# Fourteen column pairs per layer in seven products, 31 pool tiles, and the accumulating loads issued at the fetch

## The chip, the cores and the metric

The kernel runs on one core of one Trainium2 chip. The metric is the device time of one execution in microseconds (us). Before the change it is 2264.33 us, the median of 3 runs (2263.88 to 2264.35).

## The reference

A trunk of two decoder layers works on 256 tokens of width 2048 in float32. Each layer is a mixer and then an MLP, each on a normalised input and each added to the residual:

```python
h = rms_norm(x, norm_mix[layer])
x = x + mixer(h)                      # layer 0: windowed attention and a state-space scan; layer 1: dilated attention
h = rms_norm(x, norm_ffn[layer])
u = h @ w_up                          # 2048 -> 8192
x = x + square(relu(u)) @ w_down      # 8192 -> 2048
```

The change lies in the two MLPs, above all in the product with `w_down`. The mixers compute the same as before.

## The kernel before

**Operands in two parts.** Every float32 operand is split into a high and a low part, and a product is made of three matmuls (high by high, high by low, low by high). ScalarE (ACT) makes the high part `whi` of a weight tile, VectorE (DVE) the low part `wlo` (`split`, and `high` and `low` in `run`). TensorE (PE) can start a tile when both are there.

**The plan.** All matrix work is one list, `plan`, of pieces. `run` (line 291) walks through it. At each piece it emits, in this order, `low` for the piece two ahead, `fetch` for the piece six ahead, `high` for the piece three ahead, and `add` for the piece four ahead, and then the matmuls. Small work (norms, relu, transposes, splits of `u`) is kept as side tasks that `tick` slips in between; `need` forces a task to its end where a piece cannot go on without it, and so puts its instructions right ahead of that piece's matmuls.

**Two kinds of pieces in the MLP.** Both take 256 rows (two k tiles) of a weight stripe 512 columns wide, which is one tile of 128 x 1024 values, 512 KB.
- A plain piece serves all 256 tokens, with 12 matmuls that are 512 columns wide. Its weight tile is `wraw`, with four buffers, loaded by SyncE's queue (SP).
- A seven piece belongs to a `Seven` (line 245). It computes, for a chunk `c` of 1024 rows of `w_down` and a pair of column stripes (a column pair), the two by two block product with seven products in the place of eight. Each product takes two pieces (halves `h`) of 6 matmuls. Blocks are called 11, 12, 21, 22 (row half, column half); the tokens are halved too. The seven are P1, P2, and Q3 to Q7.

A column pair of a chunk takes 96 matmuls in plain pieces and 84 as a `Seven`. The price of a `Seven` is sums. Sums of operand blocks (`s1`, `s2`, then `sh`, `sl`) are made once per chunk in `operands`. Sums of weight blocks are made in two ways: `add` lets DVE add two tiles (for Q6 and Q4), and `accumulate` has GpSimd's queue (POOL) issue a DMA that loads a block from `w_down` and adds it to a tile that is there already (block 12 onto tile 11 and block 22 onto tile 12, for both halves: four such DMAs per column pair). `evict` adds each finished product to the residual `res` (7 DVE additions of 128 x 512 per column pair).

**What sets the order before.** `LOADS` says which blocks a product fetches: P1 fetches 11, P2 fetches 21, 12 and 22, in SP's order. Both accumulating DMAs are issued from `low` (line 331): the one onto 11 follows the low part of P1, which is the last reader of the plain block 11, and the one onto 12 follows the low part of P2. Q6 comes third, and its sum needs tile 11 with its accumulation done.

**The chunks.** There are eight chunks per layer. `w_up` is consumed in 16 units of 8 plain pieces. After the first two units, each chunk's seven pieces are mixed with the following units' pieces by `mixed` (line 1036): `for c, n in enumerate((20, 20, 8, 20, 20, 24, 0))` gives each chunk `n` plain pieces, of which the first four or five come ahead of the seven pieces. Before, chunks 0, 1, 3, 4 and 5 take both column pairs as `Seven`; chunks 2 and 6 take one, and their other pair is done in plain pieces (`down`); chunk 7 is plain. That is 12 per layer.

**The tile pool.** `work` has 29 tiles of 4 KB per partition: weight blocks of the `Seven`s (`sraw`), `uf`, `uh`, `ul`, the sums, and all mixer tiles. A tile is taken again when its last reader is done.

Of the kernel before, what the change touches and what calls it, by code (L numbers as in the profile page):

```python
# [15 lines left out]
T = 256  # L16
# [4 lines left out]
W = 512  # L21
# [19 lines left out]
def trunk(ctx: ExitStack, tc: tile.TileContext, x, norm_mix, norm_ffn, w_up, w_down, ab_w_in, ab_q_norm,  # L41
# [48 lines left out]
    nc.scalar.preload_act_table(AF.Exp)  # L90
    cst = consts.tile([128, C_ALL], F32, name="cst")
    par0 = w4([32, 128], "par0")
# [39 lines left out]
    cbm = cst[:, C_CB:C_CB + 128]  # L132
    mask0 = cst[:, C_M0:C_M0 + 384]
    mask1 = cst[:, C_M1:C_M1 + 384]
    mult1 = cst[:, C_N1:C_N1 + 384]
    cwT = consts.tile([128, 96], F32, name="cwT")
# [98 lines left out]
    def unit(*a, **k):  # L235
# [3 lines left out]

    SEVEN = (("P1", "a", "11"), ("P2", "b", "21"), ("Q6", "a", "t2"), ("Q7", "c", "12"), ("Q5", "a", "11"),  # L240
             ("Q4", "c", "21"), ("Q3", "a", "22"))
    LOADS = {"P1": ("11",), "P2": ("21", "12", "22")}
    SUMS = {"Q6": ("t2", "11", "22"), "Q4": ("21", "21", "t2")}

    class Seven:


        def __init__(self, w, rows, c0, kts, operands, to, needs, mark):
            self.w, self.rows, self.c0, self.operands, self.to, self.needs, self.mark = \
                w, rows, c0, operands, to, needs, mark  # L250
# [8 lines left out]
        def fetch(self, p, h):  # L259
            for b in LOADS.get(SEVEN[p][0], ()):  # L260
                r, c = self.rows[int(b[0]) - 1] + h * KC, self.c0 + (int(b[1]) - 1) * W
                nc.sync.dma_start(self.tile(b, h),
                                  self.w[r * 128:(r + KC) * 128, c:c + W].rearrange("(k p) c -> p k c", p=128))

        def add(self, p, h):
# [4 lines left out]

        def accumulate(self, p, h):

            o = {"P1": ("11", 0), "P2": ("12", 1)}.get(SEVEN[p][0])
            if o is not None:
                r, c = self.rows[o[1]] + h * KC, self.c0 + W
                nc.gpsimd.dma_start(self.raw[o[0], h],  # L276
                                    self.w[r * 128:(r + KC) * 128, c:c + W].rearrange("(k p) c -> p k c", p=128),
                                    accum_op=OP.add)

# [3 lines left out]
        def evict(self, p):  # L283

            name, b, _ = SEVEN[p]
            t, j, op = {"P1": (0, 0, OP.add), "P2": (0, 0, OP.add), "Q6": (1, 0, OP.add), "Q7": (1, 1, OP.subtract),
                        "Q5": (1, 1, OP.subtract), "Q4": (1, 0, OP.add), "Q3": (0, 1, OP.subtract)}[name]
            r = self.to[t][j]
            V.tensor_tensor(r, r, self.bank[b], op=op)

    def run():
# [54 lines left out]
        high(AHEAD)  # L346
        nc.sync.dma_start(cst[:, C_TRI:], shapes[:, C_TRI:])
        pending = []
        before = ps = None
        kept, held = [], []  # L350
        for i, (u, c) in enumerate(todo):
# [9 lines left out]
            if isinstance(u, Seven):  # L361
# [7 lines left out]
                sp = u.bank[b]  # L369
                xh, xl, t0 = u.operands(name)  # L370
                tick(True)
                for k in range(KC):
                    q = h * KC + k
                    wh, wl = xh[:, q, t0:t0 + 128], xl[:, q, t0:t0 + 128]
                    PE.matmul(sp, wh, hi[:, k], start=new and k == 0, stop=False, skip_group_check=True)
# [247 lines left out]

    def residual_unit(w, ktiles, j, needs={}, nm=None, last=None, check=None, mark=None):
        def after(ps):
            if check is not None:
                check()
            add_stripe(ps, j, last)
            if nm is not None:
                nm.begin(j)  # L630
# [15 lines left out]
    v0 = consts.tile([128, 2, 2, 64], F32, name="v0")  # L646
    k0T = consts.tile([128, 2, T], F32, name="k0T")
    dt = consts.tile([128, 2, 32], F32, name="dt")
# [6 lines left out]
    cumd = dram.tile([32, 2, 128], F32, name="cumd")  # L655
    btok = consts.tile([128, 4, 128], F32, name="btok")
    dtx = small.tile([128, 2, 32], F32, name="dtx", bufs=1)
# [293 lines left out]
    def mlp(layer, nm, nxt, last=None):  # L951
# [60 lines left out]
        def down(c, j):  # L1012
# [5 lines left out]

            def whole():
                assert all(("down", layer, k, j) in done or ("down", layer, k, j - j % 2) in done for k in range(NC - 1))  # L1020

            return residual_unit(wd, kts, j, {4 * b: ("u", layer, 2 * c + b) for b in range(2)}, nxt, last, whole).pieces

        def seven(c, j):
            def parts(name):
                i, k, t = {"P1": (0, 0, 0), "P2": (0, 1, 0), "Q4": (0, 1, 128), "Q5": (1, 0, 0), "Q6": (1, 0, 128),
                           "Q7": (1, 1, 0), "Q3": (1, 1, 128)}[name]
                return (sums[c][k] if i else u[2 * c + k]) + (t,)

# [3 lines left out]
                         {0: ("u", layer, 2 * c), 1: ("u", layer, 2 * c + 1), 2: ("sums", layer, c)},  # L1033
                         marks[c][-1]).pieces

# [28 lines left out]
    oh, ol = [None] * 4, [None] * 4  # L1064

    def dilated(g):
        boxes = [[], []]
        vb = []

        def after_qk(i, ps):  # L1070
            side(heads_T(n2, ps, R_QK + 2 + i, "qk"[i], boxes[i]), ("qk", g, i))
            if i == 1:
# [99 lines left out]
```

## Time and profile before

| what | value |
|---|---|
| median of 3 runs | 2264.33 us |
| the profiled execution's own time | 2264.74 us |
| span of its instructions on the core | 2262.9 us |
| granted TensorE clock | 1.00 |
| TensorE matmul busy | 2247.2 us, 99% |
| VectorE busy | 1749.7 us, 77% |
| ScalarE busy | 1290.0 us, 57% |
| GpSimd busy (it only issues DMAs) | 125.7 us, 6% |
| moved by DMA | 475.10 MB, of it 50.48 MB by GpSimd's queue |

The span runs from the first instruction to the last; the 1.8 us between it and the execution's own time lie outside. `L71` stands for every instruction that goes through the recording helper at line 71, so groups are told apart by their tiles. A matmul of 512 columns is listed with 0.39 us, but matmuls overlap in the array, and the pitch from one to the next is what counts. `q0` is GpSimd's DMA queue, `q1` SyncE's. The first layer's MLP lies at about 480 to 1130 us, the second's at about 1570 to 2263 us.

### The profile page before, as it was taken

The numbers are of one execution on the slowest core, as the hardware profiler recorded it, in microseconds if no ns is written. First come the engines' busy times: TensorE is split into PE (matmuls) and PEld (weight loads), VectorE is DVE, ScalarE is ACT, GpSimd is POOL, SyncE is SP. The second block draws the span as 40 slices with busy tenths as digits, with TensorE's granted clock in tenths as the row PEclk, the third lists the DMA queues.
The fourth block names the chain that finished last, engine by engine and source line by source line (L and its number), as shares of the span: only waits on it lengthen the run. The fifth ranks groups of instructions, "written<-read, shape, count | busy, mean of one in ns | idle before, by whom it ended". The sixth has DMA issues, their size and how long they took to land.

```text
span 2262.9 us, 30235 instructions
## 1 busy us (share of the span) xinstructions
PE 2247.2 (99%) x11029; PEld 1873.0 (83%) x11029; DVE 1749.7 (77%) x2482; ACT 1290.0 (57%) x1615; POOL 125.7 (6%) x116
## 2 busy tenths in 40 slices
PE   8999999999999999999999999999999999999999
PEld 7998988888888888888788778778888888888877
DVE  6779986556888888887976766665588888888786
ACT  6565545445666556565664555555566665656663
POOL 1000000000001010000000000000000000010000
PEclk9999999999999999999999999999999999999999
DMA  7546555568797797888756455546788789797874
GB/s 235 163 142 190 177 177 182 190 186 246 216 296 214 209 288 222 242 245 234 219 171 192 149 158 168 168 151 186 245 237 240 206 242 281 207 282 228 248 222 141
DMA packets 255318, 475.10 MB, mean 210 GB/s; under 512 B 17156, under 2 KB 27696, under 8 KB 255168
## 3 DMA queue, kind: packets, MB, share of 16 engines
q1 hardware_dynamic: 218976, 416.34, 56.7%
q0 software_dynamic: 26624, 50.48, 12.5%
q10 hardware_dynamic: 9568, 6.34, 0.9%
q8 instruction: 86, 1.41, 0.2%
q14 instruction: 64, 0.52, 0.1%
HBM read 470.97 MB, written 2.13 MB: 209 GB/s over the span
## 4 chain that ended last, share of the span: by engine, by line
PE 97%; DMA 1%; DVE 1%; issue 1%; ACT 0%; SPq 0%; DVEq 0%; POOLq 0%; ACTq 0%
PE acc L71 71%; PE sp L71 20%; PE uT L71 1%; PE sc L71 1%; PE o L71 1%; DMA sraw<-in_w_down_dram 1%; PE pT L71 1%; PE yp L71 1%; PE xT L71 1%; DVE wlo L71 1%; DMA wraw<-in_ab_w_in_dram 0%; PE qp L71 0%; DMA res<-in_x_dram 0%; PE yo L71 0%; PE kp L71 0%
## 5 line engine op out<-in xcount | busy, mean ns | idle before, releaser
L71 ACT ACTIVATE whi<-wraw 128x1024 fp32r<-128x1024 f32 (+1 forms) x600 | 631.9, 1054 | 493.6 <-PE acc L71 350.8
L71 DVE TENSOR_TENSOR wlo<-wraw,whi 128x1024 fp32r<-128x1024 f32 (+1 forms) x600 | 725.0, 1214 | 233.7 <-PE acc L71 159.7
L71 PE MATMUL acc<-whi,hThi 128*128 128x512 f32 (+1 forms) x1632 | 647.7, 397 | 1.8 <-ACT hThi L71 1.7
L71 PE MATMUL acc<-whi,hTlo 128*128 128x512 f32 (+1 forms) x1632 | 634.8, 389 | 1.0 <-DVE hTlo L71 1.0
L71 PE MATMUL acc<-wlo,hThi 128*128 128x512 f32 (+1 forms) x1632 | 634.1, 389 | 0.7 <-DVE wlo L71 0.7
L71 ACT ACTIVATE whi<-sraw 128x1024 fp32r<-128x1024 f32 x336 | 353.7, 1059 | 292.4 <-DVE sraw L71 137.0
L71 DVE TENSOR_TENSOR wlo<-sraw,whi 128x1024 fp32r<-128x1024 f32 x336 | 408.8, 1221 | 85.3 <-PE acc L71 35.3
L71 PEld LDWEIGHTS acc<-whi,hThi 128*128 128x128 f32 x1632 | 307.6, 188 | 66.8 <-issue 5.8
L71 PEld LDWEIGHTS acc<-whi,hTlo 128*128 128x128 f32 x1632 | 307.2, 188 | 65.7 <-DVE hTlo L71 1.8
L71 PEld LDWEIGHTS acc<-wlo,hThi 128*128 128x128 f32 x1632 | 307.9, 189 | 60.9 <-DVE wlo L71 1.1
L276 POOL DMA_DIRECT2D sraw<-in_w_down_dram x96 | 117.3, 1576 | 2058.7 <-DVE wlo L71 1815.6
L71 PE MATMUL sp<-wlo,sh 128*128 128x512 f32 x384 | 149.5, 389 | 0.0
L71 PE MATMUL sp<-whi,sl 128*128 128x512 f32 x384 | 149.5, 389 | 0.0
L71 PE MATMUL sp<-whi,sh 128*128 128x512 f32 x384 | 149.4, 389 | 0.0
L71 DVE TENSOR_TENSOR sraw<-sraw 128x1024 f32<-128x1024 f32 x96 | 117.1, 1219 | 26.4 <-DMA sraw<-in_w_down_dram 26.3
L71 DVE TENSOR_TENSOR res<-res,sp 128x512 f32<-128x512 f32 x168 | 114.7, 682 | 17.4 <-PE sp L71 17.1
L71 PE MATMUL acc<-hThi,whi 128*128 128x256 f32 x384 | 112.3, 293 | 0.0
L71 PE MATMUL sp<-whi,ul 128*128 128x512 f32 x288 | 112.1, 389 | 0.0
L71 PE MATMUL sp<-whi,uh 128*128 128x512 f32 x288 | 112.0, 389 | 0.0
L71 PE MATMUL sp<-wlo,uh 128*128 128x512 f32 x288 | 112.0, 389 | 0.0
L71 PE MATMUL acc<-hThi,wlo 128*128 128x256 f32 x384 | 108.5, 283 | 0.0
L71 PE MATMUL acc<-hTlo,whi 128*128 128x256 f32 x384 | 108.5, 283 | 0.0
(221 smaller groups left out, 2749.8 us busy)
## 6 DMA issues: line engine op xcount, KB each, us to landing
wraw<-in_w_up_dram SPq DMA_DIRECT2D x256, 512.0 KB, 5.2
sraw<-in_w_down_dram SPq DMA_DIRECT2D x192, 512.0 KB, 8.1
wraw<-in_ab_w_in_dram SPq DMA_DIRECT2D x96, 512.0 KB, 3.7
sraw<-in_w_down_dram POOLq DMA_DIRECT2D x96, 512.0 KB, 10.7
wraw<-in_c_w_qkv_dram SPq DMA_DIRECT2D x96, 512.0 KB, 4.2
wraw<-in_w_down_dram SPq DMA_DIRECT2D x64, 512.0 KB, 4.2
wraw<-in_ab_w_out_dram SPq DMA_DIRECT2D x48, 512.0 KB, 3.7
wraw<-in_c_w_o_dram SPq DMA_DIRECT2D x32, 512.0 KB, 3.6
```

What stands on the lines that cost most here:

```text
L71: return f(out, *a, **k)
L276: nc.gpsimd.dma_start(self.raw[o[0], h], self.w[r * 128:(r + KC) * 128, c:c + W].rearrange("(k p) c -> p k c", p=128), accum_op=OP.add)
```

## The change

- Chunks 0 to 6 now take both column pairs as `Seven`, 14 per layer, and the plain pieces are spread as `(18, 17, 17, 18, 17, 17, 8)`. Chunk 7 stays plain, and the second pair of chunk 6 is mixed with it.
- Q7 and Q6 change places. P1 fetches blocks 12 and 11, P2 blocks 21 and 22. The accumulating DMA onto tile 12 is issued in `fetch`, right behind the load of tile 12; the one onto 11 stays behind the low part of P1.
- Of the even `u` block of chunks 0 to 6 only the first 128 tokens are split, with high and low part in one tile (`uhl`), since plain pieces no longer read it.
- The pool grows from 29 to 31 tiles. `cst` shrinks to 384 columns; the masks become pool tiles (`mask0`, and `masks`, which is loaded when layer 1's first attention unit is done), and `k0T` and `btok` become the two halves of a pool tile `kb`.
- A stripe's next norm (or its store) begins when both the last `Seven` and chunk 7's plain unit of that stripe are done (`early`, `ready`).

```diff
-    work = ctx.enter_context(tc.tile_pool(name="work", bufs=29))
+    work = ctx.enter_context(tc.tile_pool(name="work", bufs=31))
...
-    SEVEN = (("P1", "a", "11"), ("P2", "b", "21"), ("Q6", "a", "t2"), ("Q7", "c", "12"), ("Q5", "a", "11"),
+    SEVEN = (("P1", "a", "11"), ("P2", "b", "21"), ("Q7", "c", "12"), ("Q6", "a", "t2"), ("Q5", "a", "11"),
              ("Q4", "c", "21"), ("Q3", "a", "22"))
-    LOADS = {"P1": ("11",), "P2": ("21", "12", "22")}
+    LOADS = {"P1": ("12", "11"), "P2": ("21", "22")}
...
                 nc.sync.dma_start(self.tile(b, h),
                                   self.w[r * 128:(r + KC) * 128, c:c + W].rearrange("(k p) c -> p k c", p=128))
+                if b == "12":
+                    self.accumulate("12", 1, h)
...
-                if isinstance(u, Seven):
-                    u.accumulate(*c)
+                if isinstance(u, Seven) and c[0] == 0:
+                    u.accumulate("11", 0, c[1])
...
-            for k in marks[c - 1] if 0 < c < NC - 2 else [("up", layer)] if c else []:
+            for k in marks[c - 1] if 0 < c < NC - 1 else [("up", layer)] if c else []:
                 yield from until(k)
-            if c == NC - 1:
-                yield from until(("uf", layer, 2 * c + 1))
             for i in (2 * c, 2 * c + 1):
                 yield from until(("uf", layer, i))
-                u[i] = slot("uh"), slot("ul")
-                split(u[i][0], u[i][1], uf[i])
+                if i % 2 == 0 and c < NC - 1:
+                    u[i] = slot("uhl")
+                    split(u[i][:, :, :128], u[i][:, :, 128:], uf[i][:, :, :128])
+                else:
+                    u[i] = slot("uh"), slot("ul")
+                    split(u[i][0], u[i][1], uf[i])
...
-        for c, n in enumerate((20, 20, 8, 20, 20, 24, 0)):
+        for c, n in enumerate((18, 17, 17, 18, 17, 17, 8)):
             x, o = ups[o:o + n], o + n
+            s = seven(c, 0) + seven(c, 2)
             if c == NC - 2:
-                x = sum((down(c, j) for j in (0, 1)), []) + sum((down(c + 1, j) for j in range(NS)), [])
-                mixed(x, seven(c, 2), 2, 19)
-            elif n == 8:
-                mixed(x + down(c, 2) + down(c, 3), seven(c, 0), 4.5, 16)
+                mixed(x, s[:9], 4, n + 4)
+                mixed(sum((down(c + 1, j) for j in range(NS)), []), s[9:], 0, 15)
             else:
-                mixed(x, seven(c, 0) + seven(c, 2), 4.5, n + (3 if n == 24 else 0))
+                mixed(x, s, 4.5, n)
```

The first place is SP's queue, at the first column pair of chunk 1 in layer 0. Before, tile 6009 is block 11 of the first half, 6044 block 11 of the second; then follow 21, 12 and 22 of the first half (6066, 6068, 6070) and of the second (6121, 6123, 6125):

```order
L262 DMA sraw_6009<-in_w_down_dram 128x2x512
L306 DMA wraw_6021<-in_w_up_dram 128x2x512
L262 DMA sraw_6044<-in_w_down_dram 128x2x512
L262 DMA sraw_6066<-in_w_down_dram 128x2x512
L262 DMA sraw_6068<-in_w_down_dram 128x2x512
L262 DMA sraw_6070<-in_w_down_dram 128x2x512
L306 DMA wraw_6095<-in_w_up_dram 128x2x512
L262 DMA sraw_6121<-in_w_down_dram 128x2x512
L262 DMA sraw_6123<-in_w_down_dram 128x2x512
L262 DMA sraw_6125<-in_w_down_dram 128x2x512
L306 DMA wraw_6161<-in_w_up_dram 128x2x512
```

In the changed kernel the same place of SP's queue has block 12 and block 11 of the first half (5967, 5970), of the second (5982, 5985), and then 21 and 22 of each half:

```order
L260 DMA sraw_5967<-in_w_down_dram 128x2x512
L260 DMA sraw_5970<-in_w_down_dram 128x2x512
L260 DMA sraw_5982<-in_w_down_dram 128x2x512
L260 DMA sraw_5985<-in_w_down_dram 128x2x512
L306 DMA wraw_6013<-in_w_up_dram 128x2x512
L260 DMA sraw_6035<-in_w_down_dram 128x2x512
L260 DMA sraw_6037<-in_w_down_dram 128x2x512
L260 DMA sraw_6062<-in_w_down_dram 128x2x512
L260 DMA sraw_6064<-in_w_down_dram 128x2x512
L306 DMA wraw_6091<-in_w_up_dram 128x2x512
```

The eight blocks and two plain tiles stand closer together, and both tiles 12 stand in front. PE takes these pieces as one plain piece after every two seven pieces, where before one and two seven pieces took turns. POOL's queue for this column pair and the next changes from the accumulations onto 11, 11, 12, 12:

```order
L276 DMA sraw_6009<-in_w_down_dram 128x2x512
L276 DMA sraw_6044<-in_w_down_dram 128x2x512
L276 DMA sraw_6068<-in_w_down_dram 128x2x512
L276 DMA sraw_6123<-in_w_down_dram 128x2x512
L276 DMA sraw_6386<-in_w_down_dram 128x2x512
```

to 12, 12, 11, 11:

```order
L274 DMA sraw_5967<-in_w_down_dram 128x2x512
L274 DMA sraw_5982<-in_w_down_dram 128x2x512
L274 DMA sraw_5970<-in_w_down_dram 128x2x512
L274 DMA sraw_5985<-in_w_down_dram 128x2x512
L274 DMA sraw_6312<-in_w_down_dram 128x2x512
```

So the first accumulation of a pair no longer waits for the low part of P1, but for the landing of tile 12. The second place is ACT's queue at the last hand-over of a layer. Before, this is the first plain piece of chunk 6, where `need` forces the split of the even `u` block (`uh_9729`), behind the weight tile `whi_9724`:

```order
L71 ACTIVATE whi_9711<-sraw_9672 128x1024
L71 ACTIVATE whi_9724<-wraw_9684 128x1024
L71 ACTIVATE uh_9729<-uf_8903 128x1024
L71 ACTIVATE relu_9733<-acc_9409,rs32_4976 128x512
L71 ACTIVATE relu_9733<-acc_9410,rs32_4976 128x512
```

In the changed kernel it is the first plain piece of chunk 7, which reads `uh_9912`:

```order
L71 ACTIVATE whi_9891<-sraw_9694 128x1024
L71 ACTIVATE relu_9896<-acc_9589,rs32_4977 128x512
L71 ACTIVATE relu_9896<-acc_9590,rs32_4977 128x512
L71 ACTIVATE uf_9899<-uT_9900 128x512
L71 ACTIVATE uf_9899<-uT_9906 128x512
L71 ACTIVATE uh_9912<-uf_9619 128x1024
```

Two relu passes and two squares of the last `w_up` unit now stand ahead of that split, with eight transposes on PE between them; they follow a run of six seven pieces in which no side task is let in.

More of the change, by code (lines that the diff above doesn't have):

```diff
@@ L269, in add, with accumulate @@
                 V.tensor_tensor(self.raw[o, h] if o != "t2" else self.tile(o, h), x, y, op=OP.add)
[L271 to L278, printed above, removed]
+        def accumulate(self, b, half, h):
+            r, c = self.rows[half] + h * KC, self.c0 + W
+            nc.gpsimd.dma_start(self.raw[b, h],
+                                self.w[r * 128:(r + KC) * 128, c:c + W].rearrange("(k p) c -> p k c", p=128),
+                                accum_op=OP.add)
         def source(self, p, h):
@@ L289, in evict @@
             V.tensor_tensor(r, r, self.bank[b], op=op)
+            if p == 6 and self.after is not None:
+                self.after()
     def run():
@@ L369, in run @@
                 sp = u.bank[b]
[L370 removed]
+                xh, xl, th, tl = u.operands(name)
                 tick(True)
@@ L1017, in down, with after, ready, sevens_end @@
                                      mark=marks[c][-1]).pieces
-            def whole():
-                assert all(("down", layer, k, j) in done or ("down", layer, k, j - j % 2) in done for k in range(NC - 1))
-            return residual_unit(wd, kts, j, {4 * b: ("u", layer, 2 * c + b) for b in range(2)}, nxt, last, whole).pieces
+            def after(ps):
+                if early[j]:
+                    add_stripe(ps, j, last)
+                else:
+                    add_stripe(ps, j)
+                early[j] += 1
+                ready(j, False)
+            return Unit([(wd, j * W, W)], kts, after,
+                        needs={4 * b: ("u", layer, 2 * c + b) for b in range(2)}).pieces
+        early = [0] * NS
+        def ready(j, stored=True):
+            if early[j] == 2:
+                if last is not None and stored:
+                    for t in range(2):
+                        last(t, j)
+                if nxt is not None:
+                    nxt.begin(j)
+        def sevens_end(j):
+            for k in (j, j + 1):
+                early[k] += 1
+                ready(k)
         def seven(c, j):
@@ L1027, in parts @@
                            "Q7": (1, 1, 0), "Q3": (1, 1, 128)}[name]
-                return (sums[c][k] if i else u[2 * c + k]) + (t,)
+                if name == "P1":
+                    return u[2 * c], u[2 * c], 0, 128
+                return (sums[c][k] if i else u[2 * c + k]) + (t, t)
             marks[c].append(("down", layer, c, j))
@@ L1033, in seven @@
                          {0: ("u", layer, 2 * c), 1: ("u", layer, 2 * c + 1), 2: ("sums", layer, c)},
-                         marks[c][-1]).pieces
+                         marks[c][-1], (lambda: sevens_end(j)) if c == NC - 2 else None).pieces
         def mixed(rest, s, start, end):
@@ L1064, in trunk @@
     oh, ol = [None] * 4, [None] * 4
+    masks = []
     def dilated(g):
@@ L1070, in after_qk @@
         def after_qk(i, ps):
+            if g == 0 and i == 0:
+                masks.append(w4([128, 2, 384], "masks"))
+                nc.sync.dma_start(masks[0], shapes[:, C_M1:].rearrange("p (a k) -> p a k", a=2))
+            mask1, mult1 = masks[0][:, 0], masks[0][:, 1]
             side(heads_T(n2, ps, R_QK + 2 + i, "qk"[i], boxes[i]), ("qk", g, i))
```

26 lines of the change are left out of this document (12 added, 14 removed).

## The prediction

> **What bounds the kernel now.** I read the page first, then the windows, then the chain that ended last.
>
> ```profile
> span 2262.9 us, 30235 instructions
> PE 2247.2 (99%) x11029; PEld 1873.0 (83%) x11029; DVE 1749.7 (77%) x2482; ACT 1290.0 (57%) x1615; POOL 125.7 (6%) x116
> 560.00:1060.00 500.00, 500.00 (x2257) 413.98 (x2257) 422.75 (x407) 307.63 (x324) 48.84 (x40) 1.00 0.83 242
> 2238.83 2.72 PE acc L71 x12
> 2241.55 1.36 PE sp L71 x6
> 2242.91 16.33 PE acc L71 x72
> ```
>
> The page says that TensorE is busy for 99% of the span, and the window over layer 0's mixed stretch (columns: PE, PEld, DVE, ACT, POOL, clock, share of the DMA engines, GB/s) that it is busy all the time there, with VectorE at 85% and the DMA engines at 83%. So the kernel is as long as its matmuls, as long as everything else arrives in time. The chain gives the pitch: 72 matmuls in 16.33 us, 0.2268 us each; a plain piece takes 2.72 us and a seven piece 1.36. The execution took 2264.74 us, 1.84 outside the span; my sum is made against 2264.74, which is 0.4 above the median.
>
> How near the mixed stretches are to not being fed shows at one place, chunk 3 of layer 1:
>
> ```profile
> 1870.91 0.37 SPq L306 DMA_DIRECT2D wraw<-in_w_up_dram  x1
> 1871.33 0.46 SPq L262 DMA_DIRECT2D sraw<-in_w_down_dram  x1
> 1872.27 0.37 SPq L306 DMA_DIRECT2D wraw<-in_w_up_dram  x1
> 1872.69 2.16 SPq L262 DMA_DIRECT2D sraw<-in_w_down_dram  x4
> 1884.84 1.20 POOL L276 DMA_DIRECT2D sraw<-in_w_down_dram  x1 [55.74 <-DVE wlo L71]
> 1888.67 0.39 PE L71 MATMUL sp<-whi,uh 128*128 128x512 f32 x1
> 1895.67 1.23 DVE L71 TENSOR_TENSOR sraw<-sraw 128x1024 f32<-128x1024 f32 x1 [4.32 <-DMA sraw<-in_w_down_dram]
> 1902.16 0.50 PE L71 MATMUL acc<-wlo,hThi 128*128 128x512 f32 x1 [0.67 <-DVE wlo L71]
> ```
>
> SP issues the first block of the column pair at 1871.33; PE begins P1 at 1888.67, a lead of 17.3 us. The first accumulation is issued at 1884.84, VectorE waits 4.32 us for it, and PE at last 0.67 us for VectorE. It is the queue of transfers, not an engine, that comes nearest to setting the pace here.
>
> **The change part by part.**
>
> *Matmuls.* Four column pairs (two per layer) go from 96 matmuls to 84: 48 fewer, times 0.2268 us: -10.9 us, all on the path. A finer bound doesn't exist, since the pitch is the same in plain and seven pieces by the rows above.
>
> *VectorE and ScalarE.* Per converted pair VectorE has 6 more low parts, 4 more sums and 3 more evictions; the narrower split of `u` takes back a half split 14 times.
>
> ```profile
> L71 DVE TENSOR_TENSOR wlo<-sraw,whi 128x1024 fp32r<-128x1024 f32 x142 | 172.7, 1221 | 41.2 <-ACT whi L71 16.2 <-PE acc L71 13.9 <-issue 8.4
> L71 DVE TENSOR_TENSOR res<-res,sp 128x512 f32<-128x512 f32 x71 | 48.4, 682 | 6.4 <-PE sp L71 6.2
> ```
>
> With 1.22 us for 1024 columns and 0.68 for 512 that is 4 x (10 x 1.22 + 3 x 0.68) - 14 x 0.54 = +49 us on VectorE. Over some 1200 us of mixed stretches it takes VectorE from 85% to 90%. I cost it at nothing: matmuls cover it. If the cover were gone, the whole 49 us less its present idle time would show; that is far off on the mean, and near only where seven pieces follow each other, as in the run of six (rival C).
>
> *The pool, the masks, `kb`.* SP's queue waits for pool tiles today:
>
> ```profile
> SPq L262 <- DVE sraw L71: 17.4, 14, 2.4
> SPq L262 <- PE acc L71: 8.6, 18, 1.3
> ```
>
> In the new order no `sraw` takes a slot whose last reader stands fewer than six pieces ahead of the fetch (before: two), so these waits largely go. They end ahead of PE's need, so nothing is gained on the path; masks and `kb` move between buffers at no cost, and the load of `masks` (384 KB) comes in a stretch without accumulations. Bounds for these: -1 to +1 us.
>
> *The hand-over to the plain chunk.* Before, the split of `u` is forced ahead of chunk 6's first plain piece:
>
> ```profile
> 1081.53 1.04 ACT L71 ACTIVATE uh<-uf 128x1024 fp32r<-128x1024 f32 x1
> 1082.47 1.25 ACT L71 ACTIVATE relu<-acc,rs 128x512 f32<-128x512 f32 x2
> 1082.62 0.50 PE L71 MATMUL acc<-whi,uh 128*128 128x512 f32 x1 [0.74 <-ACT uh L71]
> 1083.94 0.50 PE L71 MATMUL acc<-whi,ul 128*128 128x512 f32 x1 [0.59 <-DVE ul L71]
> 643.49 0.60 ACT L71 ACTIVATE uf<-uT 128x512 f32<-128x512 f32 x1 [0.69 <-PE uT L71]
> 1080.56 1.06 ACT L71 ACTIVATE whi<-wraw 128x1024 fp32r<-128x1024 f32 x1 [0.29 <-PE sp L71]
> ```
>
> It costs 0.74 + 0.59 = 1.33 us per layer. Now the same split is forced ahead of chunk 7's first piece, with two relu passes, eight transposes and two squares in front. ACT can begin when PE frees a `whi` buffer, at the start of the last seven piece (call it 0). `whi` ends at 1.2, the relu passes at 2.5; PE, done with its piece at 1.36, waits 1.1; transposes and squares follow one another until 4.4, the split until 5.4, when PE could have been at 2.3 (1.36 and 0.9 for the eight transposes). That is 3.1 us late, and `ul`, one more 1.22 behind, adds 0.7: 3.9 us, less the 1.33 that goes: +2.6 per layer, +5.2 in all. Bounds: 0 (side tasks could sit in other gaps) and +10 (VectorE late after six seven pieces). Queued behind it on ACT are `uh` of the second block and the `whi` of pieces three ahead, which have time.
>
> *The loads of a column pair.* This is the term that decides. Order on SP: 12, 11, 12, 11, a plain tile, 21, 22, 21, 22, a plain tile; PE wants that last plain tile after six pieces: two seven, plain, two seven, so 4 x 1.36 + 2.72 = 8.2 us behind P1. At 17.3 us lead PE reaches it 25.5 us after the first issue; ACT's and VectorE's parts (1.06 + 1.22) must come first, so it has to land by 23.2. It is the tenth tile. What the queues move is in the DMA view, for three stretches:
>
> ```profile
> q1 hardware_dynamic: 1462, 2.83, 88.9%
> q1 hardware_dynamic: 1558, 3.00, 104.0%
> q0 software_dynamic: 475, 0.94, 72.0%
> q1 hardware_dynamic: 460, 0.89, 38.2%
> ```
>
> The first row is 1871 to 1881, the second 1881 to 1889, the last two 1894 to 1901 (packets, MB, share of 16 engines). Alone, SP's queue moves 3.00 MB in 8 us: 1.40 us per tile of 0.524 MB. Beside an accumulation both queues get the same number of packets, 475 and 460: a tile then takes 4.1 us and an accumulation 3.9. An accumulation issued at 1884.84 has no packet before 1889: over 4.2 us from issue to start.
>
> Now the ledger, from the first issue. In the first 10 us 2.83 MB, 5.4 tiles, go through, one of them the plain tile from 1870.91: 4.4 of the ten are in. Tile 12 has landed by about 5.5 (estimate from the same row), its accumulation is issued then and starts at 10; the second follows; those onto tile 11 are issued behind P1's low parts, some 4 us ahead of P1 as at 1884.84, so at 13.5 and 15, and start before the first two are done at 17.8. So four accumulations fill 10 to 25.6 without a gap, and 15.6 / 4.1 = 3.8 tiles pass beside them. The remaining 1.8 tiles take 2.5 us: the tenth lands at 28.1, 4.9 us late. Before, the accumulations started at 17.7, behind nine tiles. I take 4.2: a transpose group between the pieces gives 0.3 of time, and the first accumulation starts below its full share. Ten of the 14 first pairs (chunks 1 to 5) have five plain pieces ahead of them and so such a lead. Chunk 0 has more:
>
> ```profile
> 526.12 0.46 SPq L262 DMA_DIRECT2D sraw<-in_w_down_dram  x1
> 547.12 0.39 PE L71 MATMUL sp<-whi,uh 128*128 128x512 f32 x1
> ```
>
> With 21.0 us its tile has to land by 26.9, and the cost is about 1, which I leave out; chunk 6 spreads its seven pieces one by one, and second pairs are fetched further ahead in a dense stretch: 0. So +42 us. Bounds per pair: 0, if the lead is in fact longer, and 6. What is late next once PE waits: nothing, for the sums of Q6 get the same 4 us.
>
> The Trainium skill (DMA: Bandwidth & Descriptors, Anatomy of one DMA) fits a DMA of this queue with 2 us plus bytes over 436 GB/s, which makes 1.2 us of transfer for 512 KB, four of them 4.8 us in the place of 15.6. By that price the tenth tile would land at about 22 us and cost nothing, and the sum would be 2258, the time of rival B below. No accumulation in this trace shows it: 3.9 us by the rows above.
>
> *Removed stalls.* Q6's sum has two pieces more of distance from its accumulation, so the 0.67 us at 1902.16 go: -0.7.
>
> Sum: 2264.74 - 10.9 + 5.2 + 42 - 0.7 = 2300.3, say 2300 us.
>
> **The rivals.** *B, the loads arrive in time.* The accumulations take their packets where SP's queue would have had slack, or those onto tile 11 are issued later than 17 us, so that the two pairs of accumulations don't meet; the tenth tile then lands at 23. For it: every plain tile of today lands well ahead of its use, and the early accumulation of tile 12 takes the long wait at 1895.67 out. Against it: the even split of packets at 1894 to 1901. It gives 2264.74 - 10.9 + 5.2 - 0.7 = 2258.3, and 2252 to 2259 with the bounds of the hand-over. It decides for faster from the point at which a first pair loses less than 0.2 us. Chance 0.30.
>
> *C, partial loss, or VectorE as the bound.* The first pairs lose 1 us instead of 4, or VectorE, at 90%, runs late behind runs of three and six seven pieces (six need 6 x 1.22 + 3 x 1.22 + 3 x 0.68 = 13.0 us by busy time against 8.2 on PE, of which its lead of some 4 us covers most). It gives 2258 + 10 = 2268, between 2260 and 2275. Chance 0.12, half of it within 0.2%.
>
> *My forecast* (first pairs wait for plain tiles behind the accumulations): 2275 to 2320, chance 0.58.
>
> That the change doesn't do what it says is no rival: the new order holds 48 matmuls fewer.
>
> **How the numbers follow.** A measurement of this kernel tells about 0.2%, 4.5 us, from no change: faster is below 2259.8, slower above 2268.9. Faster takes B, 0.30; the same half of C, 0.06; slower the rest, 0.64. The range holds B from 2252, C, and the forecast up to 2314, which leaves out its upper end and B's lower one. The likeliest case's own range is 2275 to 2320.
>
> **What would show it.** Right: PE idle time of 2 to 6 us in chunks 1 to 5, in the first 30 us of their seven pieces, ended by VectorE's `wlo<-wraw`, behind an ACT wait for `wraw<-in_w_up_dram`; accumulations starting some 10 us behind a pair's first load; about 4 us of idle at each hand-over, ended by `uh` and `ul`. The wait of `sraw` sums for DMAs shrinks. Wrong: PE busy without gaps in those places, with plain tiles landing 23 us behind the first issue, and a time near 2255; or idle time ended by `sraw` sums, which would put VectorE or Q6 in the place of the plain tiles.

## The result, and the profile after

The changed kernel takes 2364.22 us (2363.01 to 2366.15, 4 runs) against 2264.34 (2263.88 to 2264.88): 1.0442 of the time before, interval 1.0424 to 1.0460. The forecast of 2300 us had the sign and the place, but less than half of the size; the result lies outside its range. The profiled execution took 2363.23 us, 98.5 more than the one before. The ratios here and below compare undisturbed executions; a single one, of 5821 us in the run with thirteen pairs, is left out of them. The page of the changed kernel:

```profile
span 2361.4 us, 30348 instructions
PE 2282.4 (97%) x10981; PEld 1886.5 (80%) x10981; DVE 1794.7 (76%) x2534; ACT 1302.3 (55%) x1639; POOL 143.3 (6%) x132
...
PE 79%; DMA 15%; DVE 3%; ACT 2%; issue 1%; SPq 0%; ACTq 0%; DVEq 0%
```

TensorE has 48 matmuls fewer and is nevertheless busy for 35 us more, and idle for 79.0 us in place of 15.7. Both are to be explained. In the chain that ended last DMA had 1% before, and now has the 15% of the last row above:

```profile
PE 97%; DMA 1%; DVE 1%; issue 1%; ACT 0%; SPq 0%; DVEq 0%; POOLq 0%; ACTq 0%
```

Who ends TensorE's idle time (total, times, longest):

```profile
PE acc L71 <- ACT whi L71: 19.7, 8, 3.8
PE acc L71 <- DVE wlo L71: 14.0, 11, 4.0
PE sp L71 <- DVE res L71: 8.7, 3, 4.2
PE sp L71 <- DVE wlo L71: 7.9, 13, 0.8
PE sp L71 <- ACT whi L71: 7.4, 4, 2.8
PE acc L71 <- ACT uh L71: 3.4, 2, 1.7
```

Some 49 of the 79 us are waits for the high or the low part of a weight tile. The first pair of chunk 1 shows how one such wait comes about. The issues of SP and POOL, then the chain of the late tile, then TensorE:

```profile
624.86 2.19 SPq L260 DMA_DIRECT2D sraw<-in_w_down_dram  x4
627.15 0.65 SPq L306 DMA_DIRECT2D wraw<-in_w_up_dram  x1
627.90 2.92 SPq L260 DMA_DIRECT2D sraw<-in_w_down_dram  x4
631.55 11.05 SPq L306 DMA_DIRECT2D wraw<-in_w_up_dram  x3
```
```profile
630.59 1.20 POOL L274 DMA_DIRECT2D sraw<-in_w_down_dram  x1 [39.45 <-issue]
633.38 1.21 POOL L274 DMA_DIRECT2D sraw<-in_w_down_dram  x1 [1.58 <-DMA sraw<-in_w_down_dram]
637.79 1.20 POOL L274 DMA_DIRECT2D sraw<-in_w_down_dram  x1 [3.21 <-DVE wlo L71]
641.43 1.20 POOL L274 DMA_DIRECT2D sraw<-in_w_down_dram  x1 [2.44 <-DVE wlo L71]
```
```profile
631.55 22.41 DMA wraw<-in_w_up_dram
...
654.06 1.06 ACT whi L71
...
655.15 1.24 DVE wlo L71
...
656.43 4.28 PE acc L71 x11
660.71 1.36 PE sp L71 x6
```
```profile
642.37 0.39 PE L71 MATMUL sp<-whi,uhl 128*128 128x512 f32 x1
...
650.29 0.50 PE L71 MATMUL sp<-whi,uh 128*128 128x512 f32 x1 [0.95 <-ACT whi L71]
651.55 0.50 PE L71 MATMUL sp<-wlo,uh 128*128 128x512 f32 x1 [0.76 <-DVE wlo L71]
...
655.17 0.80 PE L71 MATMUL acc<-whi,hThi 128*128 128x512 f32 x1 [2.19 <-ACT whi L71]
656.43 0.80 PE L71 MATMUL acc<-wlo,hThi 128*128 128x512 f32 x1 [0.46 <-DVE wlo L71]
...
657.45 0.63 PE L71 MATMUL acc<-whi,hThi 128*128 128x512 f32 x1
657.88 0.63 PE L71 MATMUL acc<-wlo,hThi 128*128 128x512 f32 x1
```

The tenth tile, issued at 631.55, needs 22.41 us and lands at 653.96, 29.1 behind the pair's first issue at 624.86. TensorE began P1 at 642.37; from 649 on it waits for one late block, and then for this tile. Then the second thing: behind the wait its matmuls stand 0.43 us apart (657.45, 657.88), where 0.2268 is the pitch. From P1 to the first matmul of the seventh piece, at 660.55 (the chain goes by ends and has 660.71), pass 18.2 us for 10.9 us of work (four seven pieces, two plain): 7.3 lost. The windows show the idle time and the granted clock of this pair, and of chunk 2 (clock is the third figure from the end):

```profile
642.40:662.40 20.00, 15.63 (x58) 11.58 (x57) 10.30 (x10) 7.16 (x8) 0.42 (x2) 0.83 0.98 291
736.00:756.00 20.00, 15.93 (x54) 11.60 (x53) 9.21 (x10) 8.33 (x10) 1.08 (x1) 0.74 0.99 286
```

The clock records of the trace hold such a spell behind nearly every long wait: half clock for 3.41 or 6.83 us, once 10.24. Half of their lengths is 43.6 us of lost clock (the mean clock is 0.982); before, there was none (1.000). The Trainium skill (TensorE: Matmul & The Clock Gate, What's actually happening) has this rule: an idle window of about 3.4 us throttles the array to half rate, and a busy one releases it. The spell lengths here agree. The idle time that brings a spell is often shorter here: the spell of 10.24 us in chunk 2 begins behind a wait of 2.06 us.

**Where the 98.5 us are.** Measured in the trace like the pair above, the first six pieces of the twelve first pairs of chunks 0 to 5 lose 6.2 to 9.1 us, 7.7 on the mean, where before they lost 0.3: 12 x 7.4, some +88. The matmuls give back 10.9. The 21 us that remain lie mostly in the two chunks 6 and their hand-overs, where TensorE idles 7.9 and 8.4 us (before 1.3 each) and has half clock.

### The profile page after: what moved, and what is told of

Same layout as the page of the kernel before. It is cut to its first block, busy times and chain, and to the rows that moved or that the text cites. A ratio compares the mean times of both kernels' runs of the same rounds, so it can differ in the third digit from the quotient of the medians.

```text
span 2361.4 us, 30348 instructions
## 1 busy us (share of the span) xinstructions
PE 2282.4 (97%) x10981; PEld 1886.5 (80%) x10981; DVE 1794.7 (76%) x2534; ACT 1302.3 (55%) x1639; POOL 143.3 (6%) x132
## 4 chain that ended last, share of the span: by engine, by line
PE 79%; DMA 15%; DVE 3%; ACT 2%; issue 1%; SPq 0%; ACTq 0%; DVEq 0%
PE acc L71 55%; PE sp L71 19%; DMA wraw<-in_w_up_dram 11%; DMA sraw<-in_w_down_dram 4%; DVE wlo L71 1%; PE sc L71 1%; PE uT L71 1%; ACT whi L71 1%; PE o L71 1%; PE pT L71 1%; PE yp L71 1%; PE xT L71 0%; DMA wraw<-in_ab_w_in_dram 0%; DVE res L71 0%; DVE sraw L71 0%
## 5 line engine op out<-in xcount | busy, mean ns | idle before, releaser
L71 DVE TENSOR_TENSOR wlo<-wraw,whi 128x1024 fp32r<-128x1024 f32 (+1 forms) x568 | 687.8, 1215 | 259.8 <-PE acc L71 150.3
L71 ACT ACTIVATE whi<-wraw 128x1024 fp32r<-128x1024 f32 (+1 forms) x568 | 597.1, 1053 | 456.2 <-PE acc L71 273.8
L71 ACT ACTIVATE whi<-sraw 128x1024 fp32r<-128x1024 f32 x392 | 412.2, 1058 | 424.9 <-DVE sraw L71 137.5
L71 DVE TENSOR_TENSOR wlo<-sraw,whi 128x1024 fp32r<-128x1024 f32 x392 | 476.1, 1223 | 128.7 <-ACT whi L71 65.7
L71 PE MATMUL sp<-whi,sh 128*128 128x512 f32 x448 | 176.8, 395 | 8.7 <-DVE res L71 8.7
L71 PE MATMUL sp<-wlo,sh 128*128 128x512 f32 x448 | 176.4, 394 | 1.1 <-DVE wlo L71 1.1
L71 PE MATMUL sp<-whi,sl 128*128 128x512 f32 x448 | 176.1, 393 | 0.0
L71 PEld LDWEIGHTS sp<-whi,sh 128*128 128x128 f32 x448 | 85.7, 191 | 28.1 <-ACT whi L71 9.1
L71 PEld LDWEIGHTS sp<-wlo,sh 128*128 128x128 f32 x448 | 85.4, 191 | 19.8 <-DVE wlo L71 1.9
L71 PEld LDWEIGHTS sp<-whi,sl 128*128 128x128 f32 x448 | 85.2, 190 | 18.0
```

The costliest lines, as they stand in the source:

```text
L71: return f(out, *a, **k)
```

## The experiments

**Which part of the change does it.** My theory was the early accumulation. The first run takes the old loads into the new kernel; the second keeps the new order of SP's queue and makes the accumulations late:

```diff
-                if b == "12":
-                    self.accumulate("12", 1, h)
...
-                if isinstance(u, Seven) and c[0] == 0:
-                    u.accumulate("11", 0, c[1])
+                if isinstance(u, Seven) and c[0] < 2:
+                    u.accumulate(("11", "12")[c[0]], c[0], c[1])
```

Both also have `SEVEN` as before (Q6 ahead of Q7), and the first one `LOADS` as before.

> The changed kernel with 14 pairs, its pool and its hand-over, but with the old order of loads (P1 fetches 11; P2 fetches 21, 12, 22), Q6 ahead of Q7 and both accumulations behind the low parts of P1 and P2. Theory (the early accumulations delay the tiles that a first pair needs, and each wait of 3 to 5 us also halves the granted clock for 3.4 to 6.8 us): the twelve waits of chunks 0 to 5 (50.6 us of idle) and their clock spells go; chunk 6 and the hand-over stay (16 us idle, 8.5 of clock, where before lost 2.7). 2264.3 - 10.9 + 16.3 - 2.7 + 8.5 = 2275 us, 2262 to 2285. Rival (fourteen pairs are too much for VectorE or for the queue in any order): idle time in the first pairs stays, over 2320 us.

> The changed kernel with its order of loads on SP's queue (12, 11, 12, 11, a plain tile, 21, 22, 21, 22, a plain tile), but the accumulations issued behind the low parts of P1 and P2 as before, with Q6 ahead of Q7. Theory (it is the early start of the accumulations): ten tiles at 1.40 us are in before the first accumulation moves, so the first pairs do not wait, 2275 us, 2262 to 2290. Rival (the order on SP's queue: blocks 12 and 22 stand ahead of tiles that are needed sooner): most of the waits stay, over 2320 us.

2300.95 us (ratio 1.0163, 1.0147 to 1.0178) and 2301.15 (1.0162, 1.0145 to 1.0179). In chunk 1 with the old loads, over 20 us from P1 on:

```profile
636.90:656.90 20.00, 19.69 (x89) 15.88 (x88) 14.35 (x14) 10.78 (x13) 2.72 (x3) 1.00 1.07 273
```

TensorE is busy and its clock is full. The first six pieces lose 0.6 and 0.5 us on the mean in place of 7.7. So what makes the first pairs wait is not the order on SP's queue, and not the fourteen pairs. It is when the accumulations start; that it isn't the swap of Q6 and Q7, which both runs take back too, shows in the run with plain loads below, which keeps the swap and loses 1.2. In all, 63 of the 100 us go, and 37 stay. The total came out 26 us above what I had expected. 15.7 us of idle and 10.2 of half clock stand in the chunks 6 and at their hand-overs. And short waits remain behind Q6's sum. For the accumulation ahead of that sum VectorE waits in the kernel with the old loads (not at all in the changed kernel):

```profile
DVE sraw L71 <- DMA sraw<-in_w_down_dram: 73.3, 44, 3.7
```

The other corner, the kernel before with nothing but the new order of products, loads and accumulations:

> The kernel before (12 pairs, its pool, its plain pieces) with nothing but the new order: P1 fetches 12 and 11, P2 21 and 22, Q7 ahead of Q6, the accumulation onto 12 issued right behind the load of 12. Theory (early accumulations): the ten first pairs of chunks 0, 1, 3, 4 and 5 of two layers lose 4.2 us of idle and some 2.9 of clock each: 2264.3 + 71 = 2335 us, 2310 to 2355. Rival (the waits come from the fourteen pairs and their spread, not from the loads): 2264 us, within 10.

2357.00 us (1.0407, 1.0389 to 1.0424). So 93 us come with the new order alone, without one pair more; but only a third stands where I had put it. First pairs lose 2.7 us on the mean. More is lost further on:

```profile
PE sp L71 <- DVE res L71: 32.8, 18, 3.0
PE acc L71 <- DVE wlo L71: 9.2, 17, 0.8
```

These 32.8 us precede Q5. Since the swap it stands right behind Q6 and adds to the same bank, so it waits for Q6's eviction. The prediction had the swap as a gain of 0.7 and nothing else.

**What makes an accumulation dear.** The same four DMAs as plain loads (weight sums left out):

```diff
-                                self.w[r * 128:(r + KC) * 128, c:c + W].rearrange("(k p) c -> p k c", p=128),
-                                accum_op=OP.add)
+                                self.w[r * 128:(r + KC) * 128, c:c + W].rearrange("(k p) c -> p k c", p=128))
```

> The changed kernel with the four DMAs per pair of GpSimd's queue as plain loads: same tiles, same bytes, same places, no addition (the weight sums are left out). Theory (an accumulation takes its packets slowly, 4.1 us a tile beside 1.40 for a plain one): fourteen tiles at 1.40 us pass in the time, the tenth lands by 24 us behind the first issue in place of 29; the waits of chunks 0 to 5 fall to under 1 us each and the clock stays up: 2270 to 2290 us. Rival (any second queue that starts early takes half of the packets, whatever it does): as the changed kernel, 2350 to 2364 us.

2283.75 us (1.0088, 1.0073 to 1.0103): as the theory had it. The queues in the changed kernel from 636 to 651, and here from 631 to 640 (packets, MB, share of 16 engines):

```profile
q0 software_dynamic: 1011, 1.97, 70.8%
q1 hardware_dynamic: 1013, 1.94, 39.1%
```
```profile
q1 hardware_dynamic: 1080, 2.09, 63.2%
q0 software_dynamic: 380, 1.43, 41.2%
```

In the changed kernel the queues take turns packet by packet (1011 and 1013). A packet of an accumulation carries 1.9 KB and takes 0.708 x 16 x 15 / 1011 = 0.17 us; a plain one of the same queue carries 3.8 KB in 0.412 x 16 x 9 / 380 = 0.16 us. The accumulation thus gives each SP packet a neighbour of the same length for half of the bytes. With plain loads the queues take turns too while such a load runs (from 631 to 632, 69 packets each), but it is through in about half the time, and SP's queue then has the engines to itself: hence 1080 against 380. With plain loads the tenth tile lands 22.8 to 24.5 us behind the first issue (in place of 28.0 to 29.4), and the first six pieces lose 1.2 us. The Trainium skill (DMA: Bandwidth & Descriptors, SWDGE vs HWDGE vs iDMA) says that a DMA engine serves its queues in rounds; the equal packet counts agree.

**What the half clock costs.** Useless matmuls fill most of the wait, in the changed kernel:

```diff
+                if (name, h) == ("P2", 0) and u.c0 == 0 and u.rows[0] < 48:
+                    for _ in range(18):
+                        PE.matmul(sp, xh[:, 0, th:th + 128], hi[:, 0], start=True, stop=False, skip_group_check=True)
```

> The changed kernel, with 18 useless matmuls of 512 columns (18 x 0.2268 = 4.08 us) ahead of P2 of the first pair in chunks 0 to 5, twelve times, 49 us of additional work on TensorE; the true matmul that follows overwrites what they leave. Theory (a wait of some 4 us costs twice: its own length, and the half clock that follows it): the useless work falls into the 50.6 us of waiting, so it costs about 3 us net, and the granted clock stays at 1.00 there, which gives back some 34 of the 44.6 us: 2364 - 34 + 3 = 2333 us, 2322 to 2345. Rival (the half clock has another cause, or is not on the path): filling a wait changes nothing, 2364 us within 6.

2355.26 us (1.0405, 1.0389 to 1.0421): neither figure. TensorE did 49 us more work and the kernel became 9 us shorter, so the clock does have a price; but I had expected 31. The same pair:

```profile
642.00:662.00 20.00, 18.85 (x85) 15.04 (x83) 10.14 (x10) 8.25 (x9) 0.61 (x2) 1.00 0.98 290
```
```profile
654.93 0.50 PE L71 MATMUL acc<-whi,hThi 128*128 128x512 f32 x1 [0.40 <-ACT whi L71]
656.19 0.50 PE L71 MATMUL acc<-wlo,hThi 128*128 128x512 f32 x1 [0.76 <-DVE wlo L71]
656.53 0.40 PE L71 MATMUL acc<-whi,hTlo 128*128 128x512 f32 x1
```

Some 6 us of lost clock are left of 43.6 (the mean clock is 0.997). But the tenth tile's first matmul comes 13.4 us behind P1 on the mean of chunks 1 to 5, exactly as in the changed kernel: until the tile is there, a slow clock costs nothing. Behind it, the first six pieces lose 6.1 in place of 7.7, and the next six 1.2 in place of 0.3, since TensorE reaches Q5 earlier and waits there for Q6's eviction (8.7 us in 3 waits in the changed kernel):

```profile
PE sp L71 <- DVE res L71: 18.7, 12, 4.2
```

Net 0.7 us per pair: of a spell only that part counts in which nothing else is late.

**The lead.** The first pairs' blocks are fetched two pieces earlier; the second run also has the mended hand-over (below) and chunk 6 spread:

```diff
+        def ahead(i):
+            for k in (i, i + 2):
+                if k < len(todo) and k not in got:
+                    u, c = todo[k]
+                    if k == i or isinstance(u, Seven) and u.c0 == 0 and c[0] < 2:
+                        got.add(k)
+                        fetch(k)
```

> The changed kernel with the early accumulations kept, but the eight blocks of each first pair fetched two pieces earlier (eight ahead in place of six), two plain pieces or 5.4 us on the clock of TensorE; nothing else moves. Theory (the accumulations hold the queue from 10 to 26 us behind the first issue, and only the lead of some 17 us is too short for that): the tenth tile still lands 28.7 us behind the first issue, but that is now 6.4 us behind P1 in place of 11.8, where it is wanted at 6.3; the first pairs lose under 1 us in place of 7.6: 2364 - 12 x 6.8 = 2282 us, 2272 to 2295. Rival (the queue is short of transfer time wherever it starts: the two plain tiles that now stand behind the blocks come late, or the pool has no tiles that early): 2320 us or more.

> The same, with the two mends of the end of a layer: the even u block of chunk 7 is split by a task of its own, and the pieces of chunk 6 are spread (two seven pieces in a row before chunk 7 in place of six, and the other 19 over 19 plain pieces in place of 15). Theory (some 21 us of the loss stand there, half of it VectorE's lateness in the run of seven pieces with the half clock behind it, half the forced split): 2282 - 16 = 2266 us, 2258 to 2274. Rival (with chunk 6 as dense as the other chunks its first pair waits for loads as they did): 2276 us or more.

2329.81 us (1.0290, 1.0276 to 1.0305) and 2325.53 (1.0265, 1.0251 to 1.0280). The lead grew from 16.9 to 22.0 us on the mean of chunks 1 to 5, but the tile then landed 32.0 us behind the first issue, not 28.7, since another plain tile goes ahead of it: 10.0 behind P1, where 6.4 had been expected. The pairs lose 5.0 us each in place of 7.7. The rival was nearer: the queue is short of time in the stretch with accumulations, wherever it begins. The mends of the layer's end took 4 us more, not 16. In that trace the first pairs lose 5.8 us each, which hides some 9 us of what the mends gave; why they lose more is not shown.

**The end of a layer.** The split of the even u block of chunk 7 in a task of its own, in the kernel with the old loads:

```diff
+        def whole():
+            for k in marks[NC - 3]:
+                yield from until(k)
+            yield from until(("uf", layer, NB - 2))
+            u[NB - 2] = slot("uh"), slot("ul")
+            split(u[NB - 2][0], u[NB - 2][1], uf[NB - 2])
```

> The kernel with the old loads (14 pairs, late accumulations) with the even u block of chunk 7 split by a task of its own, when chunk 5 is done, so that relu, transposes and split of the last w_up unit no longer stand ahead of chunk 7's first plain piece. Theory (that wait, 15.7 us of idle and 10.2 of half clock in both layers, is the order of the side tasks): 2301 - 26 + 3 = 2278 us, 2272 to 2284. Rival (VectorE and ScalarE are late after the run of seven pieces, whatever is forced there): 2290 us or more.

2291.65 us (1.0120, 1.0107 to 1.0134): 9.3 us less, not 23, and the rival's figure. The order of the forced tasks was part of it; 2.3 us of waiting for `uh` and `ul` stayed at each hand-over, so the split still comes late. And in the changed kernel, chunk 6 spread:

```diff
-                mixed(x, s[:9], 4, n + 4)
-                mixed(sum((down(c + 1, j) for j in range(NS)), []), s[9:], 0, 15)
+                mixed(x, s[:9], 3, n)
+                mixed(sum((down(c + 1, j) for j in range(NS)), []), s[9:], 0, 19)
```

> The changed kernel with the pieces of chunk 6 spread: nine seven pieces stand over the last five of the eight w_up pieces in place of four, so that two of them and not six stand in a row, and the other 19 over 19 plain pieces in place of 15. Theory (VectorE, with 1.9 us of work per seven piece against 1.36 on TensorE, falls behind in the run of six; the wait of 4.2 us in the second half of chunk 6 and the half clock behind it are that, twice): 2364 - 13 = 2351 us, 2345 to 2356. Rival (the wait there is for loads too): 2360 us or more.

2355.15 us (1.0400, 1.0387 to 1.0414): 9 us less. In the changed kernel TensorE waits there for VectorE, which is busy without a gap:

```profile
1140.36 0.47 PE L71 MATMUL sp<-whi,sh 128*128 128x512 f32 x1 [4.18 <-DVE res L71]
```
```profile
1132.12 3.49 DVE L71 TENSOR_TENSOR wlo<-sraw,whi 128x1024 fp32r<-128x1024 f32 x3
1135.53 0.69 DVE L71 TENSOR_TENSOR res<-res,sp 128x512 f32<-128x512 f32 x1
1136.12 1.23 DVE L71 TENSOR_TENSOR wlo<-sraw,whi 128x1024 fp32r<-128x1024 f32 x1
1137.26 1.23 DVE L71 TENSOR_TENSOR sraw<-sraw 128x1024 f32<-128x1024 f32 x1
1138.39 1.23 DVE L71 TENSOR_TENSOR wlo<-wraw,whi 128x1024 fp32r<-128x1024 f32 x1
1139.53 0.69 DVE L71 TENSOR_TENSOR res<-res,sp 128x512 f32<-128x512 f32 x1
```

With the pieces spread, the wait of 4.2 us is gone in layer 0 and 1.2 in layer 1; waits of 1.9 and 2.3 us for relu passes come in its place. The dense run is not all of it. Just ahead of it ACT, and VectorE behind ACT, waited for loads of chunk 6's first pair:

```profile
1118.17 1.06 ACT L71 ACTIVATE whi<-wraw 128x1024 fp32r<-128x1024 f32 x1 [4.53 <-DMA wraw<-in_w_up_dram]
1122.15 1.06 ACT L71 ACTIVATE whi<-sraw 128x1024 fp32r<-128x1024 f32 x1 [2.91 <-DMA sraw<-in_w_down_dram]
```

Spreading shrinks these waits too (2.2 and 0.8 us in layer 0, where the changed kernel has 2.2, 4.5 and 2.9), so this run doesn't separate the two. With plain loads in the place of the accumulations, and the same dense run, the waits for the eviction are 2.2 and 2.7 us in place of 4.2. Whether VectorE's work or only the eviction's place behind it was too much, the last two runs ask:

```diff
+            for f in pending:
+                f()
+            pending = []
             if i:
                 low(i + AHEAD - 1)
...
-            for f in pending:
-                f()
-            pending = []
```

> The changed kernel, where a finished product's eviction is emitted ahead of the low part and the sum of later pieces, in place of behind them. VectorE does the same work. Theory (Q5 stands right behind Q6 since the swap of Q6 and Q7 and writes the same bank, so TensorE waits for Q6's eviction, and that stands behind 2 to 4 operations of 1.2 us on VectorE): the two waits of 4.2 us in chunk 6 and their half clock go, about 2364 - 11 = 2353 us, 2347 to 2357. Rival (VectorE is behind by its whole work there): the wait stays or moves to the next low part, 2360 us or more.

> The same in the kernel with 12 pairs and the new order. Theory (the bank shared by Q6 and Q5): most of the 32.8 us that TensorE waits for evictions go: 2357 - 28 = 2329 us, 2322 to 2338. Rival (VectorE's work): 2350 us or more.

2383.27 us (1.0523, 1.0507 to 1.0539) and 2352.23 (1.0386, 1.0369 to 1.0404). In chunk 6 the wait stayed at 3.2 us of 4.2: there VectorE is behind with more than the eviction, and my theory fell. In the twelve-pair kernel the 32.8 us did go down to 14.0, as expected of the shared bank, but the time hardly moved: the first pairs then lost 4.3 us in place of 2.7, 19 us in all. And the changed kernel became 19 us slower, which neither theory had. The likely reason, argued from the order and not tried by itself: with the eviction ahead, a low part ends later, and it is the low part that gives SP its next `wraw` buffer. The lead did shrink: P1 now begins 15.4 to 16.4 us behind a pair's first issue in chunks 1 to 5 in place of 16.6 to 17.5, and the first six pieces lose 8.9 us in place of 7.7, 14 us in all; chunk 6's first pairs lose 3.4 in place of 0.7.

**Is there a version that beats both?** Thirteen pairs with late accumulations, and first pairs that are less dense at their start:

```diff
+            at = [start + (end - start) / n * k for k in range(n)]
+            if n == 28:
+                at = [start + 0.75 * k if k < 6 else start + 4.5 + (end - start - 4.5) / 22 * (k - 6) for k in range(28)]
```

> Thirteen pairs per layer: the kernel with the old loads and late accumulations, but chunk 6 and the hand-over as in the kernel before (one pair and plain pieces), chunks 0 to 5 with both pairs and 18, 18, 18, 18, 18 and 22 plain pieces. 24 matmuls fewer than before are 5.4 us. Theory (with late accumulations the loads still leave short waits that grow with the share of seven pieces; 14 pairs keep some 25 us of them outside the hand-over): half of these, so 2264.3 - 5.4 + 6 = 2265 us, 2259 to 2275. Rival (without the early accumulations the pairs cost nothing but their matmuls): 2259 us within 1.5.

> The kernel with 14 pairs, old loads, late accumulations and the mended hand-over, where the first six seven pieces of a chunk's 28 stand on 4.5 plain pieces, in place of about 2.7, and the other 22 closer together. Theory (what is left is Q6's sum, which waits for accumulations issued behind P1's low part; some 4 us more between P1 and Q6 take it away): 2291.7 - 12 x 1.4 = 2275 us, 2268 to 2281. Rival (VectorE is the bound of what is left, and falls behind in the denser rest): 2288 us or more.

> The same spacing in the kernel with 13 pairs. Theory: its loss of 14 us against 2259 is mostly the same wait, 10 first pairs at 1.2 us: 2273 - 12 = 2261 us, 2257 to 2266. Rival (VectorE in the denser rest): 2271 us or more.

2273.23 us for thirteen (1.0038, 1.0024 to 1.0052), 8 above the figure expected; spaced, 2284.01 for fourteen (1.0091, 1.0068 to 1.0113) and 2269.53 for thirteen (1.0030, 1.0017 to 1.0043). The spaced kernels scatter (2278 to 2295, and 2267 to 2289). By the medians spacing gives 4 to 8 us, less than expected and less than this scatter, and in some chunks of the profiled executions waits of 2 to 4 us ahead of plain pieces came back. None beats the kernel before, so none is offered.

## Why the prediction was wrong in size

- *What bounds the kernel; matmuls.* Right: 10981 against 11029, the pitch away from the waits is unchanged.
- *The loads of a first pair.* The mechanism was right, and its times nearly so: accumulations 10 us behind the first issue (630.59 issued, 4.5 to the first packet), the tenth tile at 28.1 forecast and 28.7 on the mean of chunks 1 to 5, and 4.7 us late where it is used (its first matmul comes 13.4 us behind P1, against 8.7 in the run with new loads and late accumulations), with 4.2 to 4.9 forecast. The step that failed is "I take 4.2", x 10 pairs = 42 us, with "What is late next once PE waits: nothing" behind it; the term measured 88, of it 75 in these ten pairs and 13 in the two of chunk 0. Three things were missing. First, behind the tile come the wait for its low part (about 1 us) and the half clock, so the pair lost 7.7. The filled kernel puts the half clock at 1.6 of it locally, and 0.7 net. Second, chunk 0 lost 7.3 and 6.2, where I had put "about 1". Its tile is 1.9 us late by landing, but behind ACT's wait for it stand the forced `sh`, and behind that VectorE's `sl`, ahead of the tile's own low part:

```profile
554.05 1.06 ACT L71 ACTIVATE whi<-wraw 128x1024 fp32r<-128x1024 f32 x1 [5.01 <-DMA wraw<-in_w_up_dram]
555.01 1.99 ACT L71 ACTIVATE sh<-s 128x1024 fp32r<-128x1024 f32 x2
```
```profile
556.09 2.36 DVE L71 TENSOR_TENSOR sl<-s,sh 128x1024 fp32r<-128x1024 f32 x2 [5.19 <-ACT sh L71]
558.36 1.22 DVE L71 TENSOR_TENSOR wlo<-wraw,whi 128x1024 fp32r<-128x1024 f32 x1
```

  Third, leads were a little shorter than the 17.3 us that I took from one chunk (16.9 on the mean).
- *VectorE, at nothing.* It did 45 us more work (49 forecast), which is covered almost everywhere. In chunk 6 it was not: 4.2 us twice. That is rival C's place, "behind runs of six seven pieces", which I had given 0 in the sum; late loads have a part in it, as shown above.
- *The hand-over, 3.9 us each.* It measured 1.7 and at most 0.5, because the last seven piece ran at half clock, behind VectorE's wait just ahead of it, and took over 2 us in place of 1.36: the relu passes were through when it ended. With the old loads it was 6.6 of idle (4.9 for a relu pass, 1.6 for the split). The term depends on what is late before it.
- *Pool, masks, removed stall.* SP's waits for `sraw` tiles ended by VectorE's sums fell from 17.4 us to 6.7, and off the path, as forecast; but all its waits ahead of block loads only from 43.5 to 35.7, so "largely go" was too much. The 0.7 us that the swap of Q6 and Q7 should give were no gain by themselves: the swap brought Q5 behind Q6 on one bank.
- *Rival B* (loads arrive in time) would have needed plain loads: without the addition the first pairs lose 1.2 us. Even so that kernel takes 2283.75 us and not 2258, since the other terms stay.

Open is how much of the 21 us in the two chunks 6 belongs to the late loads of their own first pairs: spreading took 9 away, no run isolates the rest. The 37 us that stay with late accumulations are 47.5 us of loss less the 10.9 that the matmuls give back: 26 in the chunks 6 and at their hand-overs, some 16 in the six pieces that begin with Q6, and 3 in the six before them.

## What to carry to other kernels

A transfer that adds in flight is cheap for the engines and dear for its neighbours in the queue: start it when the loads that are needed first are in. Price a wait not at the lateness of the tile, but up to the point where the work is back in step: what is queued in order behind the waiting instruction on each engine comes next, and the clock after it. And a mend on one engine may delay what another's queue waits for: an eviction of 0.7 us, moved ahead of the low parts, cost 19, likely in this way.

## What the runs showed of the hardware

- Packets of an accumulating DMA carry 1.9 KB in 0.17 us; plain ones of the same queue 3.8 KB in 0.16 us.
- In the changed kernel, behind waits that together take some 2 to 5 us, TensorE's clock is at half for 3.41 us or a multiple; the pitch is then 0.43 us. Lost clock is not lost time: 38 us of it less, with useless work in the waits, made the kernel 9 us faster.
